# Moving operands of two fused transformer blocks placed 64 bytes lower, modulo 256, than the weights they meet

## The chip, the core and the metric

The kernel runs on one core of a Trainium2 chip. The metric is the device time of one execution in microseconds. The inputs are one sequence of 256 tokens of width 2048 in fp32 and some 490 MB of fp32 weights, which are read once from HBM.

## The reference

Two blocks follow each other. The first is a gated delta-rule mixer with cross attention to a memory of 256 rows; the second is a pooling mixer beside a sparse attention, and then a layer of 128 x 128 experts of which each token takes 16 for each of 8 heads.

```
h    = rms_norm(x);  proj = h @ dn_w_in                  # 2048 -> 12,336 columns
mix  = gated delta rule over 24 heads (conv, silu, chunked triangular solve)
xa   = cross attention to rms_norm(mem) @ mem_w_kv
x    = x + (concat(mix, xa) * silu(z)) @ w_out           # 4096 -> 2048

proj = x @ w_in_2                                        # pool, q, k, v, indexer
h    = layer_norm(ALPHA * x + concat(pool, attention) @ w_out_2)
qh   = h @ peer_wq; s1, s2 = qh . sub_keys; top 16 of s1 + s2 per head -> expert, gate
act  = gelu(h . u[expert])
out  = layer_norm(ALPHA * h + sum over experts of gate * act * v[expert])
```

The kernel does not gather experts. It multiplies h with all 16,384 rows of u, builds a dense matrix G of gates, and multiplies G * gelu(...) with all rows of v.

## The kernel before, in words

Every large product is made in fp32 precision out of matmuls on the type fp32r, with both operands split in a high and a low part: a * b is taken as ah * bh + ah * bl + al * bh, three matmuls for one. The tiles with h and l at the end of their names are these parts.

**Weights.** A class `Stream` reads the packed weights in granules of 128 x 1024 fp32 (512 KB). SP issues the DMA into `wraw`, ScalarE copies it to `wh` (rounded to fp32r), VectorE subtracts and writes `wl`. There are three such sets, `wraw0..2`, `wh0..2` and `wl0..2`, in the pool `w`; until the stage of the experts a fourth one is lent from the pool `wx` (`wrawx`, `whx`, `wlx`).

**Loops.** `wstat` and `wide` hold a 128 x 128 piece of the weights in the array as the stationary operand, and stream the activations past it as the moving operand of 256 tokens; `xstat` and `out_mm` do it the other way round: a piece of the activations is stationary, and 512 columns of the weights move. The inner loop of `wstat`:

```
for i, (a, b) in enumerate(((wh, xh), (wh, xl), (wl, xh))):
    pe.matmul(out=pt[:, c * 256:(c + 1) * 256], lhsT=a[:, k, :], rhs=b[:, kk, :],
              start=(kk == 0 and i == 0), stop=(kk == nk - 1 and i == 2))
```

`lhsT` is the stationary operand, and each matmul has its own load of it; `rhs` is the moving one. In the rows, `bank<-hl,wh` is a matmul that streams `hl` past weights from `wh`, and `bank<-wh,hl` one that streams `wh` past weights from `hl`.

**Stages.** Memory projection (`mh`, `ml` stationary); projection of the first block with `hh`, `hl` moving, with the delta rule beside it; its output product with `hh`, `hl`, `yh`, `yl` stationary; projection of the second block with `gh`, `gl` moving (and stationary for v); output product of the second block with `hh`, `hl` stationary; queries of the experts and the 256 granules of u with `hh`, `hl` moving, with routing and gates beside them; the 256 granules of v, with pieces of G stationary (`eog`, `eghl`, `eoj`, `ewg`).

**Order.** The order on each engine is written by the program when it is built. Small work beside the large products (norms, delta rule, routing) stands in generators in a list `sides`; `pump()` lets them go on after every few matmuls, at times that a planned clock gives. [...] All calls go through one helper, so that all rows have its line, L122. In the delta rule, `inverts` makes a triangular inverse on GpSimd (tiles `Lb`, `Xs`, `itmp`) with small DMAs before and behind it, VectorE transposes the result into `XTg`, and TensorE's merge then uses it.

**Where tiles stand.** A tile of a pool begins where the one before it ends, rounded up to 32 bytes; so the order and the sizes of tiles set each one's start, counted in bytes within a partition. In the program as built, `wh0..2`, `wl0..2`, `whx`, `wlx`, `mh`, `ml`, `yh`, `yl`, and the pieces of G begin at 128 modulo 256. `hh` begins at 53,888 and `hl` at 70,272, which is 128 modulo 256 as well; `gh` begins at 156,192 and `gl` at 172,576, which is 32 modulo 256. Pieces of these tiles lie at multiples of 512 or 1024 bytes behind their start, so that all pieces of a tile have the same remainder.

Of the kernel before, what the change touches and what calls it, by code (L numbers as in the profile page):

```python
# [10 lines left out]
F32 = mybir.dt.float32  # L11
F32R = mybir.dt.float32r
BF16 = mybir.dt.bfloat16
U32 = mybir.dt.uint32
I32 = mybir.dt.int32
AF = mybir.ActivationFunctionType
OP = mybir.AluOpType
# [8 lines left out]
NV = 24  # L26
XH = 4
# [109 lines left out]
def tile_blocks(ctx, tc, P, out, dbg=None, stop=None):  # L137
# [12 lines left out]
    def copy_act(out, in_):  # L150
        act.activation(out=out, in_=in_, func=AF.Copy)

    def tt(out, a, b, op):
        dve.tensor_tensor(out=out, in0=a, in1=b, op=op)

    def ts(out, a, s1, s2=None, op0=OP.mult, op1=OP.add):
        if s2 is None:
            dve.tensor_scalar(out=out, in0=a, scalar1=s1, scalar2=None, op0=op0)
        else:
            dve.tensor_scalar(out=out, in0=a, scalar1=s1, scalar2=s2, op0=op0, op1=op1)  # L160
# [26 lines left out]
    def put(*ts_):  # L187
        for t in ts_:
            s, side, _ = held.pop(id(t))
            side_held[0] -= side  # L190
            free.append(s)

    def get(n=1):

        while side_held[0] + n > cap[0] or len(free) < n:
            yield
        b = [_take(1) for _ in range(n)]
        return b if n > 1 else b[0]
# [10 lines left out]
    granules, start = [], {}  # L209
# [5 lines left out]
    ws = Stream(nc, act, dve, wpool, granules, 3, 3)  # L215
# [6 lines left out]
    def rsqrt_dve(y, z, wk):  # L222

        ts(wk.bitcast(U32), z.bitcast(U32), 1, None, op0=OP.logical_shift_right)
        ts(y.bitcast(I32), wk.bitcast(I32), -1.0, float(0x5F3759DF))
        for _ in range(3):
# [33 lines left out]
    def on(engines="", lat=0.3):  # L260

        t = max([clk["P"]] + [clk[e] for e in engines]) + lat
        while clk["P"] < t:
            yield

    def spare(e, us):

        while clk[e] > clk["P"] + us:
            yield
# [113 lines left out]
    hs = ExitStack()  # L383
    ctx.callback(hs.close)
    hp = hs.enter_context(tc.tile_pool(name="hp", bufs=1))
    hh = hp.tile([128, KT, T], F32R, name="hh")
    hl = hp.tile([128, KT, T], F32R, name="hl")
    wx = ExitStack()
    ctx.callback(wx.close)
    ws.lend(wx.enter_context(tc.tile_pool(name="wx", bufs=1)), start.get("w_q", len(granules)))  # L390
    b1 = ExitStack()
    ctx.callback(b1.close)
    p1 = b1.enter_context(tc.tile_pool(name="p1", bufs=1))
# [148 lines left out]
    def bc(ap, shape):  # L542
        return ap.to_broadcast(shape)

    gsm = {n: p1.tile([128, NV, 2], F32, name="g_" + n)
           for n in ("g", "beta", "gc", "E", "nE", "dec", "w0", "w1", "w2")}
    adt = p1.tile([128, 2, NV], F32, name="adt")
    act.dma_start(out=adt, in_=bass.AP(tensor=P["adt"].tensor, offset=P["adt"].offset,
                                       ap=[[0, 128], [NV, 2], [1, NV]]))
# [80 lines left out]
            act.activation(out=yv, in_=pv, func=AF.Silu)  # L630
        xdone.add(c0)

    rqx = p1.tile([128, 2, XH], F32, name="rqx")
    zqx = p1.tile([128, 2, XH], F32, name="zqx")

    def cross_scale():
        while state["ssx"] < XH or not state["kvm"] or state["kv"] < 8:
# [480 lines left out]
    x1p = x1s.enter_context(tc.tile_pool(name="x1p", bufs=1))  # L1118
# [2 lines left out]
    yh = p2.tile([128, 16, T], F32R, name="yh")  # L1121
    yl = p2.tile([128, 16, T], F32R, name="yl")
    p2.tile([128, 24], F32, name="gap")
    gh = x1p.tile([128, KT, T], F32R, name="gh")
    gl = x1p.tile([128, KT, T], F32R, name="gl")

# [383 lines left out]
    rp = rs_.enter_context(tc.tile_pool(name="rp", bufs=1, side="right"))  # L1510
    ghl = rp.tile([128, 2, T], F32R, name="ghl")
    for tag, n in (("og2", 1), ("oj", 2), ("wg", 2)):
        for _ in range(n):
            rp.tile([128, (2 if n == 1 else 1) * T], F32R, name="e" + tag, tag=tag, bufs=n)
    rp.tile([128, 8], F32, name="gap")
    pickT = rp.tile([128, 2, T], BF16, name="pickT")
    iof = rp.tile([128, 128], BF16, name="iof")
    pool.iota(iof, pattern=[[1, 128]], base=0, channel_multiplier=0, allow_small_or_imprecise_dtypes=True)

    def carve(b0, shape, dt=F32):  # L1520

        n = int(np.prod(shape))
        v = G[:, b0:, :].rearrange("p b t -> p (b t)")[:, :n]
        if dt != F32:
            v = v.bitcast(dt)
        if len(shape) > 1:
            names = "abcde"[:len(shape)]
            v = v.rearrange("p (%s) -> p %s" % (" ".join(names), " ".join(names)),
                            **{names[j]: shape[j] for j in range(1, len(shape))})
        return v  # L1530
# [3 lines left out]
    vals = carve(106, [2, 8, 2, 16])  # L1534
    idxs = carve(104, [2, 8, 2, 16], U32)
    best = carve(103, [2, 8, 16])
    pos = carve(102, [2, 8, 16], U32)
    cand = carve(101, [16, 16])
# [13 lines left out]
    def top16(v, ix, src, work):  # L1552
        dve.max(out=v[:, 0:8], in_=src)
        dve.max_index(out=ix[:, 0:8], in_max=v[:, 0:8], in_values=src)
        dve.match_replace(out=work, in_to_replace=v[:, 0:8], in_values=src, imm_value=-3e38)
        dve.max(out=v[:, 8:16], in_=work)
        dve.max_index(out=ix[:, 8:16], in_max=v[:, 8:16], in_values=work)
# [4 lines left out]
    def route():  # L1562
        for h in range(8):
            while st4["q"] <= h:
                yield
            ps = yield from get()
            for t in range(2):
                for f in range(2):
                    pe.matmul(out=ps[:, (2 * t + f) * 128:(2 * t + f) * 128 + 128],
                              lhsT=qp[:, 2 * h + f, t * 128:t * 128 + 128], rhs=sk[:, f, :], start=True, stop=True)  # L1570
            yield
            s = ssb[h % 2]
            copy_act(s, ps.rearrange("p (t f k) -> p t f k", t=2, f=2))
            put(ps)
            yield from on("A")
            for t in range(2):
                for f in range(2):
                    top16(vals[:, t, h, f, :], idxs[:, t, h, f, :], s[:, t, f, :], wrk[:, :128])
                    yield from spare("V", SV)
                tt(cand, bc(vals[:, t, h, 0, :, None], [128, 16, 16]), bc(vals[:, t, h, 1, None, :], [128, 16, 16]), OP.add)  # L1580
                top16(best[:, t, h, :], pos[:, t, h, :], cand.rearrange("p a b -> p (a b)"), wrk)
                yield from spare("V", SV)

        dve.tensor_copy(out=idf, in_=idxs)
        sm = rp.tile([128, 2, 8], F32, name="smg")
        for t in range(2):
            tt(pk[:, t, 2, :].rearrange("p (h r) -> p h r", h=8), best[:, t], bc(best[:, t, :, 0:1], [128, 8, 16]), OP.subtract)
        act.activation(out=pk[:, :, 2, :], in_=pk[:, :, 2, :], func=AF.Exp)
        pf = pos.rearrange("p t h r -> p t (h r)")
        ts(pab[:, 1].bitcast(U32), pf, 15, None, op0=OP.bitwise_and)  # L1590
        ts(pf, pf, 4, None, op0=OP.logical_shift_right)
        dve.tensor_copy(out=pab[:, 0], in_=pf)
        yield
        dve.reduce_sum(out=sm, in_=pk[:, :, 2, :].rearrange("p t (h r) -> p t h r", h=8), axis=AX.X)
        dve.reciprocal(out=sm, in_=sm)
        dve.tensor_copy(out=pab[:, 1], in_=pab[:, 1].bitcast(U32))
        for t in range(2):
            g = pk[:, t, 2, :].rearrange("p (h r) -> p h r", h=8)
            tt(g, g, bc(sm[:, t, :, None], [128, 8, 16]), OP.mult)
        yield  # L1600
        eq4 = eq.rearrange("p (h r) a -> p h r a", h=8)
        for t in range(2):
            for f in range(2):
                tt(eq, bc(iof[:, None, :16], [128, 128, 16]), bc(pab[:, f, t, :, None], [128, 128, 16]), OP.is_equal)
                yield from spare("V", SV)
                tt(eq4, eq4, bc(idf[:, t, :, f, None, :], [128, 8, 16, 16]), OP.mult)
                yield from spare("V", SV)
                dve.reduce_sum(out=pk[:, t, f, :], in_=eq, axis=AX.X)
                yield from spare("V", SV)
        for t in range(2):  # L1610
            ps = yield from get()
            for j in range(3):
                pe.transpose(out=ps[:, j * 128:j * 128 + 128], in_=pk[:, t, j, :], identity=ident)
            yield
            sl = slice(t * 128, t * 128 + 128)
            copy_act(pickT[:, :, sl], ps[:, :256].rearrange("p (j t) -> p j t", j=2))
            copy_act(ghl[:, 0, sl], ps[:, 256:384])
            dve.follow("A")
            tt(ghl[:, 1, sl], ps[:, 256:384], ghl[:, 0, sl].bitcast(F32), OP.subtract)
            put(ps)  # L1620
        yield
        sides.append(gate())
# [84 lines left out]
    def u_done(c0, m, pt):  # L1707
# [13 lines left out]
        st4["ib"] = c0 + 2  # L1721

    sides.append(route())
    wide(1, hh, hl, KT, lambda c, m, pt: q_done(c + 8, m, pt))
    if stop == "route":
# [250 lines left out]
```

## Time and profile before

| | us |
|---|---|
| median of 3 runs (2876.63 to 2881.84) | 2877.76 |
| the profiled execution's own time | 2873.15 |
| its span, from the first to the last instruction | 2871.4 |
| TensorE busy with matmuls, 19,455 of them | 2832.3 |
| VectorE busy | 1898.9 |
| ScalarE busy | 1595.7 |
| GpSimd busy | 281.0 |
| mean granted clock of TensorE | 0.994 |

The span is what the rows below are counted in; the profiled execution took 1.75 us more than its span, and 4.6 us less than the median of the three runs. [...]

### The profile page before, as it was taken

What the parts mean: (1) busy time and instruction counts of PE and PEld (TensorE: products, weight loads), DVE (VectorE), ACT (ScalarE), POOL (GpSimd) and SP (SyncE); (2) the same over time, 40 slices, a digit from 0 to 9 for tenths busy, and PEclk for the clock granted to TensorE, in tenths of its full rate; (3) what the DMA queues carried; (4) which work ended last, traced back from release to release, by engine and by line L of the source; (5) the groups of instructions that cost most, each with busy time, mean ns of one, the idle gap of its engine ahead of it and who ended that gap; (6) DMA issues with size and microseconds to landing.
All of it is one profiled execution on the core that took longest, in us unless ns stands there. A gap on an engine that the chain in (4) does not pass through costs nothing.

```text
span 2871.4 us, 50349 instructions
## 1 busy us (share of the span) xinstructions
PE 2832.3 (99%) x19455; PEld 2612.8 (91%) x19455; DVE 1898.9 (66%) x3506; ACT 1595.7 (56%) x2758; POOL 281.0 (10%) x595
## 2 busy tenths in 40 slices
PE   9999999999999899999999999999999999999998
PEld 7999999999888898879999999999997888888886
DVE  5746677765554555657888777777775655565555
ACT  6455566665643444444444777676765454545543
POOL 0001555555000000000000000000001000000000
PEclk9999999999999999999999999999999999999999
DMA  8646555555666665446556555555657766666664
GB/s 295 185 127 181 174 166 172 171 165 159 194 188 170 185 195 177 148 153 202 177 176 184 169 171 178 175 175 171 177 170 249 218 196 194 191 197 192 193 195 139
DMA packets 148432, 523.55 MB, mean 182 GB/s; under 512 B 19144, under 2 KB 20728, under 8 KB 147680
## 3 DMA queue, kind: packets, MB, share of 16 engines
q1 hardware_dynamic: 135504, 490.27, 56.5%
q0 software_dynamic: 8864, 20.81, 2.9%
q10 hardware_dynamic: 3824, 9.26, 0.9%
q8 instruction: 152, 2.49, 0.4%
q14 instruction: 88, 0.72, 0.1%
HBM read 512.84 MB, written 7.36 MB: 181 GB/s over the span
## 4 chain that ended last, share of the span: by engine, by line
PE 82%; DMA 3%; POOL 2%; DVE 1%; issue 1%; ACT 1%; POOLq 0%; ACTq 0%; DVEq 0%
PE bank L122 82%; POOL Xs L122 1%; DMA wrawwraw<-in_w_in 1%; POOL itmp L122 1%; DMA wrawwraw<-in_w_v 1%; DMA Xg<-scr_x 0%; DMA Lb<-scr_l 0%; ACT wh L122 0%; DMA wrawwraw<-in_w_out 0%; DVE wl L122 0%; DMA scr_x<-Xs 0%; DVE small L122 0%; DVE hres L122 0%; POOL scr_x L122 0%; POOL Lb L122 0%
## 5 line engine op out<-in xcount | busy, mean ns | idle before, releaser
L122 DVE TENSOR_TENSOR wl<-wrawwraw,wh 128x1024 fp32r<-128x1024 f32 (+1 forms) x837 | 1021.7, 1224 | 737.5 <-ACT wh L122 731.6
L122 ACT ACTIVATE wh<-wrawwraw 128x1024 fp32r<-128x1024 f32 (+1 forms) x837 | 881.1, 1057 | 881.2 <-PE bank L122 773.3
L122 PE MATMUL bank<-hh,wh 128*128 128x256 f32 x3376 | 964.4, 286 | 1.1 <-ACT hh L122 1.1
L122 PE MATMUL bank<-hl,wh 128*128 128x256 f32 x3376 | 956.1, 283 | 0.0
L122 PE MATMUL bank<-hh,wl 128*128 128x256 f32 x3376 | 956.0, 283 | 0.0
L122 PEld LDWEIGHTS bank<-hh,wh 128*128 128x128 f32 x3376 | 648.6, 192 | 2.6 <-ACT hh L122 1.4
L122 PEld LDWEIGHTS bank<-hl,wh 128*128 128x128 f32 x3376 | 648.7, 192 | 0.5 <-DVE hl L122 0.2
L122 PEld LDWEIGHTS bank<-hh,wl 128*128 128x128 f32 x3376 | 648.4, 192 | 0.0
L122 DVE TENSOR_TENSOR wlx<-wrawx,whx 128x1024 fp32r<-128x1024 f32 x96 | 118.4, 1233 | 103.1 <-ACT whx L122 103.0
L122 ACT ACTIVATE og<-oi,ghl 128x128 fp32r<-128x128 bf16 x512 | 162.9, 390 | 32.2 <-PE bank L122 31.5
L122 ACT ACTIVATE whx<-wrawx 128x1024 fp32r<-128x1024 f32 x96 | 101.5, 1058 | 133.1 <-PE bank L122 102.5
L122 PE MATMUL bank<-wh,eog 128*128 128x512 f32 x512 | 147.4, 389 | 0.3 <-ACT wh L122 0.3
L122 PE MATMUL bank<-wh,eghl 128*128 128x512 f32 x512 | 147.5, 389 | 0.0
L122 PE MATMUL bank<-wh,ewg 128*128 128x512 f32 x512 | 147.4, 389 | 0.0
L122 PE MATMUL bank<-wh,eoj 128*128 128x512 f32 x512 | 147.4, 389 | 0.0
L122 PEld LDWEIGHTS bank<-wh,eog 128*128 128x128 f32 x512 | 96.0, 188 | 20.6 <-ACT wh L122 0.8
L122 PEld LDWEIGHTS bank<-wh,eghl 128*128 128x128 f32 x512 | 96.1, 188 | 20.4 <-ACT wh L122 0.5
L122 PEld LDWEIGHTS bank<-wh,ewg 128*128 128x128 f32 x512 | 96.1, 188 | 19.9
L122 PEld LDWEIGHTS bank<-wh,eoj 128*128 128x128 f32 x512 | 96.0, 188 | 20.0
L122 PE MATMUL bank<-gh,wh 128*128 128x256 f32 x392 | 112.2, 286 | 0.8 <-ACT wh L122 0.8
L122 PE MATMUL bank<-gh,wl 128*128 128x256 f32 x392 | 110.5, 282 | 0.8 <-DVE wl L122 0.8
L122 PE MATMUL bank<-gl,wh 128*128 128x256 f32 x392 | 110.4, 282 | 0.0
(393 smaller groups left out, 4574.9 us busy)
## 6 DMA issues: line engine op xcount, KB each, us to landing
wrawwraw<-in_w_u SPq DMA_DIRECT2D x256, 512.0 KB, 3.8
wrawwraw<-in_w_v SPq DMA_DIRECT2D x256, 512.0 KB, 4.2
wrawwraw<-in_w_dn SPq DMA_DIRECT2D x134, 512.0 KB, 4.0
wrawwraw<-in_w_out SPq DMA_DIRECT2D x73, 512.0 KB, 3.6
wrawwraw<-in_w_in SPq DMA_DIRECT2D x61, 512.0 KB, 4.1
wrawx<-in_w_dn SPq DMA_DIRECT2D x44, 512.0 KB, 3.6
wrawwraw<-in_w_q SPq DMA_DIRECT2D x32, 512.0 KB, 4.0
wrawwraw<-in_w_kv SPq DMA_DIRECT2D x23, 512.0 KB, 5.7
```

The lines of the kernel that those rows point to most:

```text
L122: return f(*a, **kw)
```

## The change

`odd`, a tile of 192 bytes, is put ahead of `hh` in the pool `hp`, so that `hh` begins at 54,080 and `hl` at 70,464: 64 modulo 256. `rzx`, a tile of 64 bytes, is put ahead of the fourth set of weights in the pool `wx`, so that `whx` and `wlx` stay at 128. A gap of 32 bytes ahead of `gh` lets `gh` begin at 156,224 and `gl` at 172,608: 64 modulo 256 too. Other tiles behind these move up by 256 bytes and keep their remainder, or are small.

The room for it is found with small tiles. `rqx` and `zqx` (scales of the cross attention) become views of `rzx`. The gates' scratch `w2`, the one-hot row of numbers `iof` and the sums `smg` become views of `odd`; `iof`, the numbers 0 to 127 that VectorE compares with the chosen experts' numbers, is kept in bytes for it and no longer in bf16. The gap behind the tiles of G's pieces grows from 32 to 96 bytes.

The order of instructions on TensorE, VectorE and SP is the same before and after; on ScalarE and GpSimd only the ends of some waits at the last stage stand otherwise. No matmul, load, copy or DMA of the large products is added or taken away.

```diff
--- before.py
+++ after.py
@@ -12,6 +12,7 @@
 F32R = mybir.dt.float32r
 BF16 = mybir.dt.bfloat16
 U32 = mybir.dt.uint32
+U8 = mybir.dt.uint8
 I32 = mybir.dt.int32
 AF = mybir.ActivationFunctionType
 OP = mybir.AluOpType
@@ -383,11 +384,14 @@
     hs = ExitStack()
     ctx.callback(hs.close)
     hp = hs.enter_context(tc.tile_pool(name="hp", bufs=1))
+    odd = hp.tile([128, 48], F32, name="odd")
     hh = hp.tile([128, KT, T], F32R, name="hh")
     hl = hp.tile([128, KT, T], F32R, name="hl")
     wx = ExitStack()
     ctx.callback(wx.close)
-    ws.lend(wx.enter_context(tc.tile_pool(name="wx", bufs=1)), start.get("w_q", len(granules)))
+    wxp = wx.enter_context(tc.tile_pool(name="wx", bufs=1))
+    rzx = wxp.tile([128, 2, 8], F32, name="rzx")
+    ws.lend(wxp, start.get("w_q", len(granules)))
     b1 = ExitStack()
     ctx.callback(b1.close)
     p1 = b1.enter_context(tc.tile_pool(name="p1", bufs=1))
@@ -542,8 +546,8 @@
     def bc(ap, shape):
         return ap.to_broadcast(shape)
 
-    gsm = {n: p1.tile([128, NV, 2], F32, name="g_" + n)
-           for n in ("g", "beta", "gc", "E", "nE", "dec", "w0", "w1", "w2")}
+    gsm = {n: p1.tile([128, NV, 2], F32, name="g_" + n) for n in ("g", "beta", "gc", "E", "nE", "dec", "w0", "w1")}
+    gsm["w2"] = odd[:, :2 * NV].rearrange("p (c t) -> p c t", t=2)
     adt = p1.tile([128, 2, NV], F32, name="adt")
     act.dma_start(out=adt, in_=bass.AP(tensor=P["adt"].tensor, offset=P["adt"].offset,
                                        ap=[[0, 128], [NV, 2], [1, NV]]))
@@ -630,8 +634,7 @@
             act.activation(out=yv, in_=pv, func=AF.Silu)
         xdone.add(c0)
 
-    rqx = p1.tile([128, 2, XH], F32, name="rqx")
-    zqx = p1.tile([128, 2, XH], F32, name="zqx")
+    rqx, zqx = (rzx[:, n, :2 * XH].rearrange("p (m h) -> p m h", m=2) for n in range(2))
 
     def cross_scale():
         while state["ssx"] < XH or not state["kvm"] or state["kv"] < 8:
@@ -1121,6 +1124,7 @@
     yh = p2.tile([128, 16, T], F32R, name="yh")
     yl = p2.tile([128, 16, T], F32R, name="yl")
     p2.tile([128, 24], F32, name="gap")
+    x1p.tile([128, 8], F32, name="gap")
     gh = x1p.tile([128, KT, T], F32R, name="gh")
     gl = x1p.tile([128, KT, T], F32R, name="gl")
 
@@ -1512,9 +1516,9 @@
     for tag, n in (("og2", 1), ("oj", 2), ("wg", 2)):
         for _ in range(n):
             rp.tile([128, (2 if n == 1 else 1) * T], F32R, name="e" + tag, tag=tag, bufs=n)
-    rp.tile([128, 8], F32, name="gap")
+    rp.tile([128, 24], F32, name="gap")
     pickT = rp.tile([128, 2, T], BF16, name="pickT")
-    iof = rp.tile([128, 128], BF16, name="iof")
+    iof = odd[:, :32].bitcast(U8)
     pool.iota(iof, pattern=[[1, 128]], base=0, channel_multiplier=0, allow_small_or_imprecise_dtypes=True)
 
     def carve(b0, shape, dt=F32):
@@ -1582,7 +1586,7 @@
                 yield from spare("V", SV)
 
         dve.tensor_copy(out=idf, in_=idxs)
-        sm = rp.tile([128, 2, 8], F32, name="smg")
+        sm = odd[:, 32:].rearrange("p (t h) -> p t h", t=2)
         for t in range(2):
             tt(pk[:, t, 2, :].rearrange("p (h r) -> p h r", h=8), best[:, t], bc(best[:, t, :, 0:1], [128, 8, 16]), OP.subtract)
         act.activation(out=pk[:, :, 2, :], in_=pk[:, :, 2, :], func=AF.Exp)
```

## Rows read from the trace of the kernel before

**Rows 1.** Busy time, share of the span and instructions of each engine.

```profile
PE 2832.3 (99%) x19455; PEld 2612.8 (91%) x19455; DVE 1898.9 (66%) x3506; ACT 1595.7 (56%) x2758; POOL 281.0 (10%) x595
```

**Rows 2.** Groups by operation and shape: xcount | busy us, mean ns | idle.

```profile
L122 PE MATMUL bank<-hh,wh 128*128 128x256 f32 x3376 | 964.4, 286 | 1.1 <-ACT hh L122 1.1
L122 PE MATMUL bank<-gh,wh 128*128 128x256 f32 x392 | 112.2, 286 | 0.8 <-ACT wh L122 0.8
L122 PE MATMUL bank<-hh,whx 128*128 128x256 f32 x352 | 102.1, 290 | 0.0
L122 PE MATMUL bank<-gh,whx 128*128 128x256 f32 x136 | 40.1, 295 | 5.5 <-ACT whx L122 5.3 <-ACT gh L122 0.2
L122 PE MATMUL bank<-wh,hh 128*128 128x512 f32 x196 | 78.0, 398 | 0.0
L122 PE MATMUL bank<-whx,hh 128*128 128x512 f32 x60 | 23.5, 392 | 0.0
L122 PE MATMUL bank<-wh,gh 128*128 128x512 f32 x48 | 19.1, 399 | 0.0
```

**Rows 3.** Timeline of TensorE, expert stage: start us, us, what.

```profile
1499.74 0.28 PE L122 MATMUL bank<-hl,wh 128*128 128x256 f32 x1
1499.86 0.28 PE L122 MATMUL bank<-hh,wl 128*128 128x256 f32 x1
...
1501.30 0.28 PE L122 MATMUL bank<-hh,wl 128*128 128x256 f32 x1
```

**Rows 4.** Timeline of TensorE, second block's projection, streaming gh and gl.

```profile
999.84 0.28 PE L122 MATMUL bank<-gl,wh 128*128 128x256 f32 x1
999.96 0.28 PE L122 MATMUL bank<-gh,wl 128*128 128x256 f32 x1
1000.07 0.28 PE L122 MATMUL bank<-gh,wh 128*128 128x256 f32 x1
...
1001.25 0.28 PE L122 MATMUL bank<-gl,wh 128*128 128x256 f32 x1
```

**Rows 5.** Timeline of TensorE, run with hh and hl as weights.

```profile
1239.72 0.39 PE L122 MATMUL bank<-wl,hh 128*128 128x512 f32 x1
...
1241.99 0.39 PE L122 MATMUL bank<-wh,hl 128*128 128x512 f32 x1
```

**Rows 6.** Timeline of TensorE, run with gh and gl as weights.

```profile
1082.63 0.39 PE L122 MATMUL bank<-wlx,gh 128*128 128x512 f32 x1
...
1084.96 0.39 PE L122 MATMUL bank<-wh,gl 128*128 128x512 f32 x1
```

**Rows 7.** Timeline of TensorE, eight short matmuls with weights from G.

```profile
1353.73 1.05 PE L122 MATMUL bank<-G 128*128 128x128 f32 x8
```

**Rows 8.** Chain that ended last, inside the delta-rule stage: start us, us, what.

```profile
276.14 1.62 POOL scr_l L122 x3
...
331.22 0.45 DVE XTg L122
```

**Rows 9.** Chain that ended last, inside the delta-rule stage, later.

```profile
708.92 0.45 DVE XTg L122
```

**Rows 10.** TensorE busy us (xcount), the same two stretches, matmuls on hh alone.

```profile
276.00:331.00 55.00, 52.84 (x291) 1.00 0.66 194
649.00:708.00 59.00, 52.88 (x283) 1.00 0.56 160
```

**Rows 11.** TensorE in the same two stretches, matmuls on hl alone.

```profile
276.00:331.00 55.00, 41.08 (x146) 1.00 0.66 194
649.00:708.00 59.00, 39.87 (x142) 1.00 0.56 160
```

**Rows 12.** PE, PEld, DVE, ACT, POOL busy us in a stretch of routing; clock, DMA.

```profile
1400.00:1480.00 80.00, 80.00 (x670) 80.00 (x670) 72.10 (x213) 33.03 (x37) 0.00 (x0) 1.00 0.60 177
```

**Rows 13.** VectorE, groups by shape.

```profile
L122 DVE TENSOR_TENSOR oj<-iof,pickT 128x256 fp32r<-128x256 bf16 x128 | 53.5, 418 | 0.0
L122 DVE TENSOR_TENSOR eoj<-G,eoj 128x256 fp32r<-128x256 f32 x64 | 26.7, 418 | 0.0
```

## The prediction

> **What bounds the kernel now.** I read the page's first part first: TensorE is busy for 2832.3 of 2871.4 us, VectorE for 66%, ScalarE for 56%, GpSimd for 10% [rows 1]. So TensorE sets the time, almost without a gap, and the change adds or removes no matmul. What it can alter is the step from one matmul to the next. I therefore grouped TensorE's matmuls by operands and shape, to see how many have a moved tile on which side [rows 2], and read the timeline for the step in a run of each kind.
>
> The reader is to see four steps there. In the expert stage, hh and hl (128 modulo 256) stream past weights at 128: 13 steps take 1.56 us, 120 ns each, and the rows look the same over hundreds of matmuls [rows 3]. In the second block's projection, gh and gl (32 modulo 256) stream past weights in the same tiles at 128, with the same code and shape: 12 steps take 1.41 us, 117.5 ns each, and single steps are 0.11 or 0.12, not all alike [rows 4]. With hh and hl as weights and 512 columns moving, 10 steps take 2.27 us, 227 ns [rows 5]; with gh and gl as weights, 2.33 us, 233 ns [rows 6]. So where a tile begins does show in the step: a base of 32 against 128 takes 2.5 ns off a matmul when it is the moving side, and adds 6 ns when it is the weights' side. A base of 64 against 128 stands nowhere in this trace; that is what has to be bounded.
>
> **The change, part by part.**
>
> *hh and hl as the moving side.* The groups [rows 2] give 3376 matmuls of `hh,wh` and 352 of `hh,whx`; each has two partners of the same count (hl with wh, hh with wl), so 3 x 3728 = 11,184. About 480 of them stand ahead of other work, and their step is set by that; I count 10,700. The bounds for the new step: from below, the loads of weights alone. Eight short matmuls of 128 columns in a row take 1.05 us [rows 7]; less one duration of at most 0.28 [rows 3], 7 steps take 0.77, 110 ns each. A step of 110 would be worth 10 x 10,700 = 107 us. From above, the worst that a base has shown: gh as weights pays 6 ns over hh, so 126, which costs 64 us. The nearest row is that of gh as the moving side, 117.5: the same code, the moving base also below that of the weights. Its steps vary, where equal bases give one value throughout; I take it that a base on the 64-byte grid of the weights settles nearer to the shorter steps, and choose 116.5: 3.5 ns x 10,700 = 37.5 us less. At 117.5 it is 26.8.
>
> *gh and gl as the moving side.* 3 x (392 + 136) = 1584 matmuls [rows 2] go from 117.5 to the same 116.5: 1.6 us less.
>
> *hh, hl, gh, gl as weights.* 3 x (196 + 60) = 768 matmuls with hh or hl [rows 2] step by 227 now. At 64 the moving weights stand 64 above them, at 32 they stood 96 above: between 0 and 6 ns more; half of it, 3 ns, costs 2.3 us (4.6 at most, nothing at least). gh and gl have 48 of one kind [rows 2] and 192 in all; from 233 to 230 they win 0.6.
>
> *What gives part of it back.* In two stretches of the delta rule the chain that ended last is not TensorE's: from 276.14 to 331.22 GpSimd inverts, with its DMAs around it, until VectorE's `XTg` [rows 8], and a second such piece ends at 708.92 [rows 9]. TensorE is full there too, but its merge waits for `XTg`; it comes there earlier and waits longer. These stretches hold 291 + 283 matmuls on hh [rows 10] and 146 + 142 on hl [rows 11]: 862 x 3.5 = 3.0 us back.
>
> *Cover.* A faster TensorE asks for granules sooner. VectorE is the next engine: in the fullest stretch, that of routing, it works 72.1 of 80 us [rows 12], 90%, and would have 93% at 116.5 / 120 of the time. It stays covered, though not at 110, where it would have 98%. DMA moves at 0.60 of its engines there [rows 12] and has room.
>
> *Bytes for iof.* VectorE's compares with a bf16 input take 418 ns for 256 elements, its subtractions with fp32 inputs of the same size 418 as well [rows 13]; the input's width is not in the price, and I put bytes at nothing. If they doubled it, 256 compares would add 107 us to VectorE over the gates, spread over the stage of the gates; VectorE, at 66% over the span [rows 1], would hide most of it. The views in `odd` and `rzx` are tiles of up to 192 bytes, and add no instruction: nothing.
>
> Sum: -37.5 - 1.6 + 2.3 - 0.6 + 3.0 = -34.4 us. The profiled execution, 2873.15 us, would take 2838.8; the runs shown lie 4.6 above it, so the median goes from 2877.76 to 2843.4. I predict 2843.
>
> **The rivals.**
>
> *No change.* Equal bases modulo 256 may not be the point: the irregular 117.5 of gh may come from a base off the 64-byte grid, or of its distance of 96, and a base at 64 may stay at 120. For it speaks that hh's step is so even, as if set by something that 64 leaves alone; against it that gh alone shows that the step is not fixed. Then hh as weights costs 0 to 4.6 us, gh loses its 2.5 ns or keeps it (at most 1584 x 2.5 = 4.0): 2874 to 2886, most likely 2879. [...]
>
> *Slower.* The two streams are read side by side, and 64 may be the distance at which they meet more often: 256 columns of the one are read beside 128 of the other, so they pass each other at any distance. Its price per matmul is that which gh shows as weights, 6 ns: 10,700 x 6 = 64 us, with 1584 x 8.5 = 13 for gh, about 2955 in all. It decides as soon as the step of hh passes 120 by more than half a nanosecond (5.4 us). For it speaks that the one base in the trace that differs is worse in one of its two roles; against it that the role in which it is better is the one that 12,768 of the matmuls have.
>
> *More than forecast.* If both streams no longer meet, the step falls to between 115 and the 110 of the loads alone: at 110, 107 + 12 for gh (7.5 x 1584) less 9 in GpSimd's stretches (862 x 10) is 110 us, of which VectorE, at 98%, would take a part. So 2768 to 2826; with a quarter of the 110 lost to VectorE, 2795.
>
> **How the numbers follow.** The forecast, a step of 115 to 118.5, has a chance of 0.50, and a range of its own from 2826 to 2867 (the same sum with these steps); more than that 0.12; no change 0.17; slower 0.21. Two tenths of a per cent, 5.8 us, is about what a measurement of this kernel can tell from no change. So faster has 0.62, same 0.17, slower 0.21. The range runs from 2795, below which lies a small part of the deeper case, to 2888, beyond which lies most of the slower case.
>
> **What would show it.** Right: in the timeline of the expert stage, hh's steps below 0.12, 13 of them in about 1.51 us; gh's steps near the same value; runs with hh as weights at 227 to 230; longer waits of TensorE for `XTg`; `oj<-odd,pickT` still at 418. Wrong: 13 steps in 1.56 (no change) or more (slower); or TensorE with many short gaps, ended by `wl` or `wh`, which would mean that VectorE or ScalarE bounds the faster stream.

## The result, and the profile after

The changed kernel took 2840.48 us (median of 4 runs, 2839.09 to 2841.78), the kernel before, beside it, 2878.35 (2876.63 to 2881.84). The ratio is 0.9867, with a 95% interval from 0.985 to 0.9884. The forecast was 2843. The profiled execution took 2839.09 us and has a span of 2837.4, 34.0 less than before.

The first part of the page answers to [rows 1]: the same 19,455 matmuls, in 48.4 us less.

```profile
PE 2783.9 (98%) x19455; PEld 2564.1 (90%) x19455; DVE 1893.3 (67%) x3506; ACT 1595.2 (56%) x2758; POOL 286.6 (10%) x595
```

The timeline of TensorE (start us, us, what) answers to [rows 3 to 6], and shows two places more: the first block's projection, and a merge of the delta rule.

```profile
99.52 0.28 PE L123 MATMUL bank<-hh,wh 128*128 128x256 f32 x1
...
100.82 0.28 PE L123 MATMUL bank<-hh,wl 128*128 128x256 f32 x1
...
102.35 0.28 PE L123 MATMUL bank<-hh,wh 128*128 128x256 f32 x1
...
325.70 0.28 PE L123 MATMUL bank<-hh,wl 128*128 128x256 f32 x1
329.20 0.31 PE L123 MATMUL bank<-XTg,lq 32*32 32x32 f32 x2 [3.22 <-DVE XTg L123]
330.34 1.06 PE L123 MATMUL bank<-XTg,lq 32*32 32x32 f32 x30 [0.84 <-DVE XTg L123]
...
331.92 0.41 PE L123 MATMUL bank<-hh,wl 128*128 128x256 f32 x1
...
335.12 0.41 PE L123 MATMUL bank<-hh,wl 128*128 128x256 f32 x1
...
725.07 0.47 PE L123 MATMUL bank<-wh,hh 128*128 128x512 f32 x1
...
999.80 0.28 PE L123 MATMUL bank<-gh,wl 128*128 128x256 f32 x1
...
1001.16 0.28 PE L123 MATMUL bank<-gh,wl 128*128 128x256 f32 x1
...
1081.62 0.39 PE L123 MATMUL bank<-wh,gh 128*128 128x512 f32 x1
...
1083.91 0.39 PE L123 MATMUL bank<-wl,gh 128*128 128x512 f32 x1
...
1236.70 0.39 PE L123 MATMUL bank<-wh,hh 128*128 128x512 f32 x1
...
1238.99 0.39 PE L123 MATMUL bank<-wl,hh 128*128 128x512 f32 x1
...
1499.46 0.28 PE L123 MATMUL bank<-hh,wh 128*128 128x256 f32 x1
...
1500.93 0.28 PE L123 MATMUL bank<-hl,wh 128*128 128x256 f32 x1
```

The reader is to see two steps where there was one. At a granted clock of 1.00 a matmul of 256 columns lasts 0.28 us in these rows and the next one starts 0.11 to 0.12 us after its start, so what is read is the step from one start to the next. In the expert stage 13 steps of hh take 1.47 us (1499.46 to 1500.93), 113 ns each; in the projection 13 steps of the same code take 1.53 us (100.82 to 102.35), 118 ns each. Before, it was 120 in the expert stage [rows 3], and 119.9 as the mean over the whole trace. gh takes 12 steps in 1.36 us, 113 ns, where it took 117.5 [rows 4]. Ten steps with hh or gh as weights take 2.29 us, 229 ns, where they took 227 [rows 5] and 233 [rows 6].

These are no accidents of short pieces. The table by windows of TensorE (us, busy and count, granted clock, DMA share, GB/s) takes one long run of each kind, and the stretch around the merge at 329 us:

```profile
100.00:150.00 50.00, 50.00 (x427) 1.00 0.62 190
1480.00:1556.00 76.00, 76.00 (x672) 1.00 0.63 197
996.00:1070.00 74.00, 74.00 (x655) 1.00 0.62 190
...
320.00:325.00 5.00, 5.00 (x45) 1.00 0.73 227
326.00:329.20 3.20, 0.00 (x1) 0.91 0.13 26
329.20:331.60 2.40, 1.56 (x33) 0.50 0.19 40
331.60:335.10 3.50, 3.50 (x17) 0.50 0.42 95
335.10:337.00 1.90, 1.90 (x55) 0.91 0.98 384
```

A count takes in the matmuls that began up to 0.28 us before the window, so the step is (50 + 0.28) / 427 = 117.8 ns in the first and (76 + 0.28) / 672 = 113.5 in the second. Over the whole trace the mean step from hh or hl to hh or hl, in pieces without an interruption, is 119.9 before and 115.5 after. A run keeps one of the two steps, 113.5 or 118, from its first few matmuls to its next interruption; among 186 runs of at least 18 steps none went over in its middle (98 kept the short step, 88 the long one).

The second reading is that of the delta rule. At 325.70 hh's stream stops, the merge waits until 329.20 for `XTg`, the granted clock falls to 0.50, and 15 steps of hh (331.92 to 335.12) take 3.20 us, 213 ns each. The same follows the waits that end at 492.26 and 707.71. The waits of TensorE (what for: us, times, longest), first of the kernel before, then of the one after:

```profile
PE bank L122 <- DVE XTg L122: 2.9, 4, 0.9
```

```profile
PE bank L123 <- DVE XTg L123: 12.7, 8, 3.2
PE bank L123 <- ACT wh L123: 7.3, 4, 5.0
PE bank L123 <- ACT whx L123: 6.6, 1, 6.6
```

Put matmul beside matmul, the change falls apart by stage as follows (from the starts of all matmuls of the two traces; from the first to the last it is 34.7 us less, and the time outside of them grows by 0.7):

| stage | before, us | after, us | change |
|---|---|---|---|
| up to the delta rule (187.5 us) | 182.4 | 180.8 | -1.6 |
| projection with the delta rule beside it | 536.1 | 539.3 | +3.2 |
| first output product (hh as weights) | 184.1 | 184.9 | +0.8 |
| second projection: gh moving, then pool and v | 278.4 | 273.6 | -4.8 |
| second output product, queries | 145.1 | 145.1 | 0.0 |
| granules of u with routing | 820.6 | 788.6 | -32.0 |
| granules of v | 709.8 | 709.5 | -0.3 |

Nearly all of the gain is in the granules of u. The delta-rule stage streams hh as well, 3588 steps of it, and got slower.

VectorE's compares with the numbers in bytes answer to [rows 13] (groups by shape of the kernel after); they take 418 ns, as with bf16:

```profile
L123 DVE TENSOR_TENSOR oj<-odd,pickT 128x256 fp32r<-128x256 uint8 x128 | 53.5, 418 | 0.0
...
L123 DVE TENSOR_TENSOR eoj<-G,eoj 128x256 fp32r<-128x256 f32 x64 | 26.7, 417 | 0.0
```

### The profile page after: what moved, and what is told of

Same layout as the page of the kernel before. It is cut to its first block, busy times and chain, and to the rows that moved or that the text cites. A ratio compares the mean times of both kernels' runs of the same rounds, so it can differ in the third digit from the quotient of the medians.

```text
span 2837.4 us, 50347 instructions
## 1 busy us (share of the span) xinstructions
PE 2783.9 (98%) x19455; PEld 2564.1 (90%) x19455; DVE 1893.3 (67%) x3506; ACT 1595.2 (56%) x2758; POOL 286.6 (10%) x595
## 4 chain that ended last, share of the span: by engine, by line
PE 70%; DMA 2%; DVE 1%; ACT 1%; issue 0%; POOL 0%; POOLq 0%; ACTq 0%; DVEq 0%
PE bank L123 70%; DMA wrawwraw<-in_w_in 1%; DMA wrawwraw<-in_w_v 1%; DVE wl L123 0%; ACT wh L123 0%; DMA wrawwraw<-in_w_out 0%; DMA wrawwraw<-in_w_q 0%; DVE small L123 0%; DVE hres L123 0%; DMA hot<-in_bucket_hot 0%; DVE pl L123 0%; ACT og L123 0%; ACT hh L123 0%; POOL hres L123 0%; ACT lg L123 0%
## 5 line engine op out<-in xcount | busy, mean ns | idle before, releaser
L123 PE MATMUL bank<-hh,wh 128*128 128x256 f32 x3376 | 951.5, 282 | 1.1 <-ACT hh L123 1.1
L123 PE MATMUL bank<-hl,wh 128*128 128x256 f32 x3376 | 942.8, 279 | 0.2 <-DVE hl L123 0.2
L123 PE MATMUL bank<-hh,wl 128*128 128x256 f32 x3376 | 942.5, 279 | 0.0
L123 PEld LDWEIGHTS bank<-hh,wh 128*128 128x128 f32 x3376 | 640.3, 190 | 2.7 <-ACT hh L123 1.5
L123 PEld LDWEIGHTS bank<-hl,wh 128*128 128x128 f32 x3376 | 638.4, 189 | 0.9 <-DVE hl L123 0.6
L123 PEld LDWEIGHTS bank<-hh,wl 128*128 128x128 f32 x3376 | 637.3, 189 | 0.1
L123 DVE TENSOR_TENSOR wlx<-wrawx,whx 128x1024 fp32r<-128x1024 f32 x96 | 118.5, 1235 | 101.9 <-ACT whx L123 99.6
```

The lines of the kernel that those rows point to most:

```text
L123: return f(*a, **kw)
```

## The experiments

Two questions: what sets the step, and where the gain of the delta-rule stage went. My theory on the first is that the remainder of the distance between the two streams, modulo 256 bytes, sets it; the rivals are that the base of hh alone does (whatever the weights' base), or that the small tiles and the bytes had a part in it. On the second I first held that the merges merely stand too early in the written order for a faster TensorE (theory G); the rival is that GpSimd's chain itself is as long as the stage, and a third that the recurrence behind the merges bounds it.

**hh back at 128, all else as after.** `odd` is taken away from ahead of hh; its contents go behind `hl`, and `w2` and `rzx` into another pool. gh stays at 64, iof in bytes.

```diff
-    odd = hp.tile([128, 48], F32, name="odd")
...
+    ob = hp.tile([128, 64], F32, name="ob")
...
-    iof = odd[:, :32].bitcast(U8)
+    iof = ob[:, :32].bitcast(U8)
```

> The changed kernel with hh and hl back at 128 modulo 256; gh and gl stay at 64, iof stays in bytes, the small tiles stay off their old places. Theory R (the distance of the moving base from the weights' base sets the step): in the expert stage 120 ns a step again, runs with hh as weights at 227, gh's steps at 114 as after the change, waits for XTg back at some 3 us; the time is that of before less what gh gains, 1500 x 3.5 ns = 5 us, so some 2873. Rival theory S (the small tiles or the bytes have a part in the gain): the time stays clearly under 2865 with 120 ns steps, or VectorE's compares differ from 418 ns.

Measured: 2872.95 us (median of 10 runs) against 2873.45, ratio 0.9993, interval 0.998 to 1.0006. The window 1491 to 1553 us lies in one long run of hh in this kernel, in the one before and in the one after:

```profile
1491.00:1553.00 62.00, 62.00 (x519) 1.00 0.59 183
```

That is (62 + 0.28) / 519 = 120.0 ns. The kernel before has 519 there too; the kernel after has 549, 113.4 ns:

```profile
1491.00:1553.00 62.00, 62.00 (x549) 1.00 0.64 198
```

hh as weights is back at 227.3. So the gain is hh's base, but for what gh won in the kernel after; bytes, views and the new order of small tiles are worth nothing that can be measured. One miss: gh's steps were expected at 114 here, but gh, with base 64 in both kernels, ran its long piece at 117.8 here and at 113.4 in the kernel after. The base allows the short step, it does not secure it.

**hh at 64 and the weights `wh0..2`, `wl0..2` at 64 too.** A tile of 192 bytes is put ahead of the pool of the weights; `whx` and `wlx` stay at 128.

```diff
+    oa = const.tile([128, 48], F32, name="oa")
...
-    odd = hp.tile([128, 48], F32, name="odd")
```

> hh and hl at 64 as in the changed kernel, but wh0..2 and wl0..2 at 64 too (the lent fourth set, and all other weights, stay at 128). Theory R (distance): 120 a step in the expert stage, though hh is at 64. Theory A (the moving operand's own remainder of 64 is what is good): 113 to 118 stay. The stage of v is a by-product: its moving operand is then at 64 past weights at 128; no matter how the step there goes from 227, it tells nothing of R against A. Time: R some 2870 plus what the stage of v adds or takes (3072 matmuls, 3 us for each ns).

Measured: 2896.47 us (one run), the slowest of the study. Its windows of TensorE: that of hh again, and one in the granules of v, where these weights move past pieces of G that stay at 128:

```profile
1491.00:1553.00 62.00, 62.00 (x519) 1.00 0.59 182
2300.00:2600.00 300.00, 300.00 (x1287) 1.00 0.64 190
```

The step of hh is 120.0 again, although hh stands at 64: equal bases, equal step. In the same trace hh streams past `whx` at 128 with a mean of 117.3. And in the granules of v, where a matmul lasts 0.39 us, the step goes from 300.39 / 1325 = 226.7 in the kernel after,

```profile
2300.00:2600.00 300.00, 300.00 (x1325) 1.00 0.65 193
```

to 300.39 / 1287 = 233.4: a difference of 64, made by moving the weights' tile and not hh, costs there 6.7 ns. The base alone explains none of the three; the distance explains all.

**The other distances.** Only hh and hl are moved; the diff is of the kind above, with other sizes of the tiles `oa` ahead of hh and `ob` behind hl, here for 192:

```diff
-    odd = hp.tile([128, 48], F32, name="odd")
+    oa = hp.tile([128, 16], F32, name="oa")
```

hh at 192, 0, 96, 160, 224 and 32:

> As the kernel above, with hh and hl at 192 modulo 256, 64 above the weights in place of 64 below. Theory R1 (only equal bases are bad; any other distance on the 64-byte grid does): steps of 113 to 118 in the expert stage, 2835 to 2850. Theory R2 (the moving base has to be below the weights'): 120 or more, 2870 or more; by the trace of gh as weights (the moving base 96 above) up to 126, so up to 2940. hh as weights: then the moving weights lie 64 below, and the step should be that of gh as weights in reverse, 227 or a little less.

> As above, with hh and hl at 0 modulo 256, 128 away from the weights on either side. R1: 113 to 118 in the expert stage, 2835 to 2850. If the pattern repeats each 128 bytes: 120, some 2873. If distance alone counts and 128 is the farthest: the shorter of the two steps after the change (113.5) everywhere, some 2820.

> Small tiles as in the kernels of the scan, hh and hl at 96 modulo 256, 32 below the weights; gh and gl at 64. So far the scan has these means of hh's step: at equal bases 119.9, at 64 below 115.5, at 128 away 119.0, at 64 above 117.7, and gh at 96 below 117.6. If the step falls evenly towards 64 below, some 117.7 here; if only the 64-byte grid has the short step of 113.5, 118 or more throughout; time 2855 to 2872.

> As above with hh and hl at 160, 32 above the weights. Theory: above the weights the short step of 113.5 is rare (at 64 above 4 of 100 steps), so 117 to 119 here, and hh as weights pays 4 to 7 ns; 2862 to 2875. Rival: every base but the equal one has some share of the short step, mean under 117, under 2858.

> hh and hl 96 above their weights, modulo 256 (224 against 128), all else as in the kernel after. Theory R, that the remainder of the distance sets the step: this is the same distance as 96 below from the weights' side (as gh as weights had before, with moving weights 96 above), so hh as weights, with moving weights now 96 below, takes about 233 ns, and the step of hh is between 116.5 and 118.5 ns, about 2856 to 2868 us. Rival: the step depends on the order of the two alone (above or below) and not on the distance: then 117.7 as at 64 above, and 2866.

> hh and hl 96 below their weights, modulo 256 (32 against 128), where gh stood in the kernel before. Theory R: hh's step is that of gh in the kernel before, 117.0 to 118.0 ns, and hh as weights takes 233 ns as gh did, so 2861 to 2869 us. Rival, that the row of gh owed its 117.5 to its stage and not to its base: hh's step is below 116 or above 119.

Measured, one run each (of the kernels before and after the medians above); the kernel before took 2873.45 us beside hh at 192 and 0, 2877.34 beside hh at 96 and 160, and 2876.14 beside hh at 224 and 32, so times of different groups compare to some 4 us only. The steps are means over the trace of all pieces without an interruption, worked out from the starts of the matmuls:

| kernel | hh less weights, bytes | time, us | hh moving: mean step, ns | matmuls from 1491 to 1553 us | hh as weights: step, ns |
|---|---|---|---|---|---|
| before | 0 | 2878.35 | 119.9 | 519 | 227.3 |
| after | -64 | 2840.48 | 115.5 | 549 | 229.1 |
| hh at 160 | +32 | 2855.79 | 116.8 | 534 | 233.2 |
| hh at 192 | +64 | 2865.76 | 117.7 | 529 | 233.3 |
| hh at 32 | -96 | 2863.84 | 118.0 | 530 | 233.4 |
| hh at 96 | -32 | 2867.59 | 118.3 | 526 | 233.2 |
| hh at 0 | +-128 | 2870.14 | 119.0 | 524 | 232.4 |
| hh at 224 | +96 | 2875.23 | 119.9 | 519 | 234.1 |

The distance sets the step in both roles, and the best of the eight is the one that the change took. The two roles do not agree: 0 is, with +96, the worst for 256 moving columns, and the best for 512. Nor is the sign free: 64 below gives 115.5, 64 above 117.7. The same distance made of other starts gives the same step: 64 below for 512 moving columns is 233.4 with the weights' tile at 64 and G's pieces at 128, and 233.3 with the weights' tile at 128 and hh at 192. And the remainder is one of 256 and not of 512: hh at 54,080 and gh at 156,224 differ by 256 modulo 512, yet in the kernel after both have steps of 113.5 and 118 as the moving side and of 229 as weights.

Where I had a number for a distance from gh in the kernel before, it held (hh at 32: 118.0 and 233.4, where gh had 117.5 and 233); the expectation of 116.5 to 118.5 for hh at 224 did not, nor did its rival's 117.7, with 119.9: there single steps go from 116 to 125 and their mean is no better than with equal bases. Of the others, hh at 96 came out on the second of its two ways (118 or more). hh at 192 has a step within R1's 113 to 118, but its time lies between R1's and R2's, and as weights it was expected at 227 or less and took 233.3. hh at 0 is nearest to a pattern of 128 bytes by its 119.0, but its 232.4 as weights against 227.3 speaks against one. hh at 160 came out by its rival's numbers, under 117 and under 2858, not by the theory's.

**The kernel after, unaltered, once more.**

> The changed kernel once more, unaltered, as the measure for the run with later merges beside it on the same chip. In its first profile a run of matmuls on hh holds one of two steps from its first few matmuls to its end, some 113.5 or some 118 ns (mean over the stage of u 115.0). Theory L (which of the two is chosen as a run begins hangs on the moment, not on the program): the same run takes the other step in some places of this profile, and the times of single executions differ by more than those of the kernel before. Rival (the program sets it): the same step in the same places.

Measured: 2842.39 us (4 runs, 2836.03 to 2845.51), ratio 0.988, 0.9863 to 0.9896; mean step of hh 115.1. Of 181 runs of hh that can be put side by side in the two traces, 174 took the same step and seven the other one. The three longest of the seven (280, 280 and 268 steps) held 117.8 in the first trace and 113.4 in this one. A window inside the first of them, in the kernel after and here:

```profile
225.00:255.00 30.00, 30.00 (x258) 1.00 0.61 178
```

```profile
225.00:255.00 30.00, 30.00 (x267) 1.00 0.63 188
```

So the program alone does not set the step, and its rival has fallen for these seven; for the other 174 the two traces don't tell the theories apart. In the delta-rule stage these three make this trace's steps 3.7 us shorter, and the two profiled executions lie 3.06 us apart; so part of the spread of the changed kernel is which of its two steps a run falls into. That it spreads more than the kernel before is not shown: 9.5 us beside 5.9 here, but 2.7 beside 5.2 in the first measurement. TensorE waited for `XTg` again, 14.5 us.

**Merges later.** The planner puts the transposes into `XTg`, and with them the merge, 4 us later behind GpSimd's inverse.

```diff
-    XD = 8.0
+    XD = 12.0
```

> The changed kernel with XD, the planned time from GpSimd's last DMAs to the merge, at 12 in place of 8, so that more matmuls on hh stand ahead of each merge in TensorE's list. Theory G (the stage of the delta rule gave its gain back, because TensorE now comes to the merges before XTg is there: waits of 12.7 us where before had 2.9, and 48 matmuls at 213 ns at half the clock behind the three longest, 4.5 us): waits for XTg under 3 us, none or few steps of 213, 10 to 16 us less than the changed kernel beside it. Rival (the chain through GpSimd and the recurrence is as long as the stage whatever the order): the wait turns up at another place of the stage, and the time stays within 4 us of the changed kernel.

Measured: 2840.25 us (4 runs), ratio 0.987, 0.9852 to 0.9887: nothing gained or lost. Its waits and its timeline:

```profile
PE bank L123 <- DVE XTg L123: 10.2, 6, 3.5
...
PE bank L123 <- ACT y L123: 6.5, 2, 6.3
```

```profile
543.42 0.28 PE L123 MATMUL bank<-hh,wl 128*128 128x256 f32 x1
549.96 1.35 PE L123 MATMUL bank<-ident,y 128*128 128x128 f32 x4 [6.26 <-ACT y L123]
```

The waits for `XTg` stay, and one of 6.26 us appears behind the merge, in the recurrence. Theory G has fallen: a later place moves the wait. Its rival is tried next.

**A shorter inverse, after and before.** Every second step of GpSimd's inverse is left out, and the planner's clock is charged for it as if it were there, so that the order on all engines stays.

```diff
-                tmp = dnp.tile([4 * NP, 128], F32, name="itmp")
...
+                if j % 2:
+                    for _ in range(2):
+                        clk["G"] = max(clk["G"], clk["P"]) + 0.2 + 2.2e-3 * n * w
+                else:
+                    tmp = dnp.tile([4 * NP, 128], F32, name="itmp")
...
```

> The kernel after, with every second step of GpSimd's triangular inverse left out (180 instructions fewer on GpSimd, about 16 of the 33 us of each of six inverses); the instructions of all other engines stand in the same order. This part of the computation is left out. Theory I, that the inverse on GpSimd with its small DMAs is what TensorE waits for in the delta-rule stage of the changed kernel: the waits for XTg fall from 12.7 us to less than 3, the stretches at the lower clock behind them go, and the time falls by 10 to 16 us below the kernel after, to 2825 to 2832. Rival P, that the stage is held by the recurrence behind the merges or by another chain as long as this one: the waits for XTg shorten but others take their place, and the time stays within 4 us of the kernel after.

> The kernel before, with the same steps of the inverse left out (this part of the computation is left out). Theory I: the kernel before waits for XTg for only 2.9 us, so it wins 0 to 3 us against the kernel before, and the distance between the two shortened kernels is 44 to 52 us where that between the two whole ones is 37. Rival P: the distance stays at 35 to 41 us.

Measured: the shortened kernel after takes 2816.66 us (4 runs), ratio 0.9789 to the kernel before, 0.9768 to 0.981; the shortened kernel before 2870.99 (10 runs), ratio 0.9978, 0.9968 to 0.9988. In the first, no wait for `XTg` is left in the list, which now begins with

```profile
PE bank L123 <- ACT wh L123: 7.0, 4, 4.9
PE bank L123 <- ACT whx L123: 6.7, 1, 6.7
PE bank L123 <- ACT x L123: 3.9, 1, 3.9
```

Between its first matmul on hh and the first of the output product, the projection with the delta rule takes 601.0 us, where the kernel after takes 725.07 - 99.52 = 625.6:

```profile
99.03 0.28 PE L123 MATMUL bank<-hh,wh 128*128 128x256 f32 x1
...
700.03 0.47 PE L123 MATMUL bank<-wh,hh 128*128 128x512 f32 x1
```

The kernel before takes 723.62 - 99.28 = 624.3 between the same two matmuls:

```profile
99.28 0.28 PE L122 MATMUL bank<-hh,wh 128*128 128x256 f32 x1
...
723.62 0.47 PE L122 MATMUL bank<-wh,hh 128*128 128x512 f32 x1
```

and the shortened kernel before 719.81 - 100.40 = 619.4:

```profile
100.40 0.28 PE L122 MATMUL bank<-hh,wh 128*128 128x256 f32 x1
...
719.81 0.47 PE L122 MATMUL bank<-wh,hh 128*128 128x512 f32 x1
```

The distance between the two shortened kernels is 54.3 us, between the two whole ones 37.9. The same change of placement is worth 18.4 us in this stage once GpSimd is quick enough, and costs 1 to 3 us there when it is not (1.2 between these two matmuls, 3.2 in the table above, whose stage begins only at 187.5 us). Theory I, that GpSimd's chain takes the gain, held, though all its numbers were too small: 10 to 16 us for the kernel after, where it wins 23.8; 0 to 3 for the kernel before, where it wins 5.2; and 44 to 52 between the two. By the profiled executions the stage is 24.5 us shorter in the shortened kernel after than in the whole one: 14.0 are stops of TensorE at the merges, 4.5 the steps at the lower clock behind them, and 3.9 three runs of hh that took 113.4 in place of 117.8. Those 3.9 are not owed to the inverse for sure, since the same three runs took the shorter step in the second profile of the kernel after as well; without them the shorter inverse is worth some 20 us.

## Why the prediction was right, and which term was not

By the two profiled executions, with the starts of all matmuls put side by side (spans: 34.0 us less):

| term of the forecast | forecast, us | measured, us |
|---|---|---|
| hh and hl moving | -37.5 | -46.9 |
| gh and gl moving | -1.6 | -4.4 |
| hh and hl as weights | +2.3 | +1.3 |
| gh and gl as weights | -0.6 | -0.9 |
| given back to GpSimd's chain | +3.0 | +17.1 |
| sum | -34.4 | -33.8 |

The sums are those of the rows shown; the other steps together are 0.9 us shorter, which gives the 34.7 from the first matmul to the last.

**What bounds the kernel.** Right: TensorE stays busy for 98% of the span, and what changed is its step. In the delta-rule stage, though, GpSimd's chain sets the time: with every second step of its inverse left out, the stage of the kernel after is 24.5 us shorter, of which 3.9 are not owed to the inverse for sure.

**hh moving.** The direction was right: a base of 64 against 128 shortens the step. Its size was taken from gh's row, 117.5, with a nanosecond off for the 64-byte grid, 116.5. In place of one value there are two, 113.5 and 118, and their mean is 115.5 over the trace and 115.0 in the granules of u (788.6 us there against 820.6). The reason given for 116.5, a base on the 64-byte grid of the weights, is not what the runs show: hh at 0 and 192 stands on that grid too and has 119.0 and 117.7, while hh at 160, off the grid, has 116.8. The irregular 0.11 and 0.12 of [rows 4] were the sign that a run may hold more than one step; I read them as noise about a mean.

**gh moving.** Right in sign; 117.6 to 114.1 in this trace. In the kernel with hh at 128 and in the one with the shorter inverse, the same gh at the same base has 117.1 and 117.0, so here the forecast of 116.5 and the measured 114.1 are both within what one base gives.

**hh, gh as weights.** 229 for both, where 230 was forecast. That 64 lies between 0 and 96 was no reason, though: with hh 64 above the weights it is 233.3.

**Given back.** This is the term that failed: 3.0 us forecast, 17.1 measured. The forecast counted 862 matmuls in the two stretches in which the chain that ended last ran through GpSimd [rows 8, 9], and multiplied them by 3.5 ns. What the runs showed in its place: GpSimd's part is as long as the stage at five of the six merges (the stops of TensorE before them last 3.5, 2.1, 3.0, 0.5 and 2.7 us), not in two. The kernel before already waits for `XTg` four times, 0.9 us at most: the chain came in so nearly together with TensorE that it had no slack at all, and what hh won in that stage (3588 steps) was waited away. The chain that ended last shows only those pieces that happened to win by a hair. And here a wait was dearer than its length: after each of the three longest stops, 2.7 to 3.5 us, the clock stands at 0.50 for the next matmuls, 213 ns instead of 113 to 118. So 13.9 us of shorter steps in this stage turned into 3.2 us more, 17.1 in all.

One thing more the forecast did not have: GpSimd itself got slower. From the first to the last of its 67 instructions the six inverses take 241.6 us together, where they took 232.1 in the kernel before (237.9 in the second profile of the kernel after). GpSimd's 595 instructions take 280.9 to 282.1 us in the four profiles in which hh's mean step is 119.7 or more, and 284.0 to 286.7 in the eight with a shorter one. So the chain that the stage waits for got longer with a faster stream. The two profiles of the kernel after lie 3.7 us apart in the six inverses, and why the spans grow was not tried.

The forecast of 2843 against 2840.48 owes its closeness to two errors that cancel, which is luck: 12 us too little won by the step, 14 too little given back.

**Cover.** Right: in the granules of u TensorE makes no stop of over 0.6 us, before or after, and VectorE has 1893.3 us of work as against 1898.9.

**Bytes.** Right, at 418 ns, and by the kernel with hh at 128.

**The rivals.** "No change" fell, with 115.5 ns for 119.9; its lower bound of 2874 us had no sum behind it, since its terms give 2877.8 to 2886.4. Where the tiles begin does matter: the step goes with the distance of the moving tile from the weights', from 115.5 to 119.9 ns and from 226.7 to 234.1. "Slower" fell for 64 below, but the kernel with the weights at 64 shows that the same rearrangement made on the other side is a loss: 2896.47 us. "More than forecast", a mean step under 115, fell with 115.5, though half of the runs hold 113.5; none holds one under 113. That two streams pass and meet, from which these two rivals argue, was my picture: the rows show matmuls and loads at work side by side, each for 80.00 of 80 us [rows 12], and no run shows how either is read. The 110 ns of the loads alone was an estimate as well, from [rows 3, 7].

**What stays open.** What in the chip makes the step depend on the distance, and what decides which of the two steps a run falls into. Both steps were seen for the same code, bases and operands; what stands ahead of a run differs, but I did not try a kernel that varies only that.

## What to carry to other kernels

Where the time is a long stream of loads and matmuls from SBUF, read the step from one start to the next for each pair of tiles, together with the tiles' starting addresses: the remainder of their distance modulo 256 bytes was worth up to 4.4 ns of 119.9 for 256 moving columns here and up to 7 of 234 for 512, costs no instruction, and has to be tried, since the best distance for 256 moving columns is a bad one for 512. Before a gain of the bounding engine is multiplied by its matmuls, look at the short waits in each stage: one that recurred with nearly nothing in it marked here a chain as long as the stage, and there the gain was worth nothing. Here the next step would be a shorter inverse: with half of it left out, some 20 us more came free, and a version that computes all of it in less time was not tried.

## What I had not expected of the hardware

- Two stable steps at one placement: 113.5 and 118 ns, held for hundreds of matmuls (672 and 427 in the windows above) from the first few of a run on. hh at 32 has two as well, 95 runs at 117 and 86 at 119 ns.
- The step depends on sign as well as distance (64 below 115.5, 64 above 117.7), and with 96 above single steps scatter from 116 to 125 ns.
- With 512 columns moving, equal bases are best (226.7 to 227.3), 64 above the weights costs 2 ns (229.1), and all other distances 5 to 7 (232.4 to 234.1).
- In the kernel after, three stops of TensorE of 2.7 to 3.5 us at the merges were each followed by a granted clock of 0.50 and 16 steps of 213 ns.
- GpSimd's same 595 instructions took 280.9 to 282.1 us beside a stream with steps of 120 ns, and 284.0 to 286.7 beside a faster one.
